# First products of the first layer from x without token factors, its norms reordered, and a down projection that ends in two halved tiles

## The chip, the cores and the metric

The kernel runs on one core of a Trainium2 chip. The metric is the device time of one execution in microseconds (us). The engines of the core are TensorE (PE: matrix products, with its weight loads listed as PEld), VectorE (DVE), ScalarE (ACT), GpSimd (POOL) and SyncE (SP, which here only starts transfers). Each engine works through its own list of instructions in order, and they wait for one another by semaphores.

## The reference

Two layers of an encoder over 512 tokens of width 1024, with 256 memory tokens. Cut to what matters here:

```
def rms_norm(x, g):
    y = x * rsqrt(mean(x * x, axis=-1) + 1e-6)
    return y * g

mem_n = rms_norm(mem, mem_norm_g)
for l in range(2):
    h = rms_norm(x, g_pre_mix[l])
    proj = h @ w_in[l]                    # 44 tiles of 128 columns
    q_a, k_a, v_a, q_b, k_b, v_b, q_m, gate_pre = split(proj)
    o_a = neighbourhood attention; o_b = dilated attention
    o_m = attention of q_m into mem_n @ w_mem_kv[l]
    merged = sum of sigmoid(gate) * (o @ w_br) over the three branches
    x = x + rms_norm(merged @ w_out[l], g_post_mix[l])
    h = rms_norm(x, g_pre_ffn[l])
    a, b = halves of conv3(h @ w_up[l])
    x = x + rms_norm((gelu(a) * b) @ w_down[l], g_post_ffn[l])
```

The norm of a token is one factor for the token (r, from the mean of its squares) times one gain for each channel (g). The factor may be applied before a product with weights or, as a scaling of columns, after it.

## The kernel before

Everything is kept transposed: x is 8 tiles of 128 channels x 512 tokens, and the tokens are worked on in two halves of 256 where a norm is near. Every product is made of three, since each float32 operand is split into a high part (hi, a rounding done as a cast on ACT) and a low part (lo, the rest, a subtraction on DVE or POOL): hi x hi, hi x lo, lo x hi (`mm3`, line 244). So each tile of weights (8 x 128 x 128, 512 KB) costs a load on SP's queue into one of three buffers (wraw), a cast on ACT (whi) and a subtraction on DVE or POOL (wlo), and each normalised tile of x costs on DVE a product with factor and gain, on ACT a cast and on DVE a subtraction (`normed`, line 340).

The order of work comes from `Woven` (line 46): PE's instructions are written out in one sequence with a clock that adds an estimated cost for each; other work is written as generator jobs that are due so many microseconds of that clock later, and `tick`, `need` and `give` let jobs in at their time or until a flag is set. So numbers such as KVD = 7.3 or LAT1 = 12.0 decide where in the lists of the engines a job's instructions stand.

What matters of the program, in order:

- Start of layer 0 (lines 835 to 848): load x's first half, two tiles of w_in, x's second half; norm of the first half; then squares of the second half, the other four tiles of the group, and the memory's norm (`mem_norm_job`, line 415) as a job.
- The group: the first six tiles of w_in (0, 3, 6, 1, 4, 7) are multiplied in pairs into six PSUM banks, first for tokens 0 to 255, then for 256 to 511 (`run_group`). Each pair of a half waits for one flag per half.
- Layer 0 then makes the memory's keys and values (`mem_kv`, four tiles of w_kv, line 442), and goes on to the projections of 512 columns, attention, gates, output projection, up projection with convolution and GELU.
- The down projection (`sublayer_end`, line 779): 8 output tiles m0 to m7, each 22 steps of three products. In layer 0, m0 to m6 are made for all 512 tokens, m7 in two halves, so that the norm of the first half can begin while the second half is multiplied. `end_job` (line 373) then scales the outputs og, adds them to x, and sums x's new squares in acc2; `pre_norm_job` of layer 1 follows (9 us of the clock later).
- The boundary to layer 1: `kv_ahead` (line 955) loads and splits w_kv's tiles and the first two of the group during m7; the memory's keys of layer 1 come behind m7; then layer 1's group.
- The memory's norm for layer 1 is spawned at the start of layer 0's down projection; its squares are made on ACT and added on POOL (MSQ = G).
- Some low parts are made on POOL: GEN = 'GGVGVG' and KVE = 'VVGG' name the engine of each group and key tile at the boundary (G is POOL, V is DVE); at the start the pairs (V, G) and (V, G, V, G) do.

In the profile line 114 is the helper through which all work of DVE and ACT is issued, so there the tiles' names tell the place. L242 is the matrix product, L253 a transpose, L192 the load of x, L225 a load of weights, L420 a load of memory tokens, L316 the addition of squares on POOL.

Of the kernel before, what the change touches and what calls it, by code (L numbers as in the profile page):

```python
# [7 lines left out]
F32 = mybir.dt.float32  # L8
# [8 lines left out]
N_MEM = 256  # L17
# [20 lines left out]
SQG, LOG, GEN, KVE = {0: (), 1: ()}, {0: (), 1: ()}, 'GGVGVG', 'VVGG'  # L38
# [4 lines left out]
KVD, GWD, NG, LAT1 = 7.3, 1.0, 2, 12.0  # L43
# [76 lines left out]
def tile_hybrid_encoder(ctx, tc, xT, memT, memg, vecs, rpb, w_in, w_kv, w_bra, w_brb, w_brm,  # L120
# [69 lines left out]
    def load_x(half):  # L190
        for k in range(0, KD, 2):
            nc.sync.dma_start(out=xs[k // 4][:, k % 4:k % 4 + 2, half], in_=xT[:, k:k + 2, half])  # L192

    load_x(HALVES[0])
# [27 lines left out]
    def weights(src, K, C, slot=None, eng=None, after=None):  # L222

        raw = wp.tile([128, K, C], F32, tag="wraw", name=nm("wraw"))
        nc.sync.dma_start(out=raw, in_=src)  # L225
# [119 lines left out]
    def raw_split(l, goff, k, src, hi, lo):  # L345

        g = vec[:, l, goff + k:goff + k + 1]
# [11 lines left out]
    def pre_norm_job(l, goff, acc, hs, i):  # L359
        half, box = HALVES[i], []  # L360
        yield from rstd_job(acc if isinstance(acc, list) else [acc[:, half]], 256, box)
        for k in range(KD):
            normed(x[k][:, half], vec[:, l, goff + k:goff + k + 1], box[0], hs[k][0][:, half], hs[k][1][:, half],
                   G if k in LOG[l > 0 and goff == V_PRE] else V)
        crit[0] = last_copy[0]
        yield 1.2
        wv.give(f"h{l}.{goff}.{i}")
# [5 lines left out]
    def end_job(l, goff, og, acc, acc2, i, then, lat, more=()):  # L373
        half, box = HALVES[i], []
        yield lat
        yield from rstd_job([acc[:, half]] + list(more), 256, box)
        for k in range(KD):
            V.tensor_mul(og[k][:, half], og[k][:, half], box[0])
            (G if then is None and i and k in TAILG else V).tensor_add(x[k][:, half], x[k][:, half], og[k][:, half])
            if acc2 is not None:  # L380
                sumsq_add(acc2[:, half], x[k][:, half], k == 0, None, G if k in SQG[goff == V_POSTF] else V)
            else:
                nc.sync.dma_start(out=out[:, k, half], in_=x[k][:, half])
        if then is not None:
            yield 9.0
            yield from then(i)

    def factor_end_job(l, goff, og, acc, acc2, i, nxt):
# [5 lines left out]
        for k in range(KD):  # L394
            V.tensor_mul(og[k][:, half], og[k][:, half], box[0])
            V.tensor_add(x[k][:, half], x[k][:, half], og[k][:, half])
            raw_split(l, gnext, k, x[k][:, half], h[k][0][:, half], h[k][1][:, half])
# [18 lines left out]
    def mem_norm_job(l, hm, slot):  # L416
# [5 lines left out]
        acc = small("h32", 3)  # L422
        for k in range(KD):
            sumsq_add(acc, raws[k], k == 0, None, MSQ if l else V)
        yield 14.0
        box = []
        yield from rstd_job([acc], N_MEM, box)
        for k in range(KD):
            t = slot(F32R, (128, 2, N_MEM))
            normed(raws[k], mg[:, k:k + 1], box[0], t[:, 0, :], t[:, 1, :])  # L430
            hm.append((t[:, 0, :], t[:, 1, :]))
        yield 1.2
# [11 lines left out]
    def mem_kv(l, hm, km, vm, pre=()):  # L444
        wv.need(f"mem{l}")
        for m in range(4):
            w = pre[m] if pre else weights(w_kv[l, m], KD, 128)
# [18 lines left out]
    def run_group(grp, hs, half, flag, cols=None, side=2):  # L466
        if flag and side == 2:
            wv.need(flag)
        n = len(hs)
        ws, pss = grp  # L470
        for i in range(0, len(ws), side):
            for k in range(n):
                if flag and side > 2:
                    wv.need(f"{flag}.{k}")
                rhs = [t[:, half] for t in hs[k]]
# [303 lines left out]
    def sublayer_end(l, goff, w_of, rhs, n_half, then, lat=(1.4, 1.8), mid=None, fill=()):  # L779
# [22 lines left out]
        ws = {m: [p() for p in w_of(m, m - n0)] for m in range(n0, KD)}  # L802
# [3 lines left out]
        for i, half in enumerate(HALVES):  # L806
            order = list(range(n0, KD) if i == 0 else range(KD - 1, n0 - 1, -1))
            while order:
# [26 lines left out]
    hs = h_tiles()  # L835
    wv.spawn(pre_norm_job(0, V_PRE, first_squares(HALVES[0]), hs, 0))
    gw = group_weights([w_in[0, m] for m in FIRST[:2]], (V, G))
# [229 lines left out]
```

## Time and profile before

| what | value |
|---|---|
| median of 3 runs | 1562.9 us (1562.28 to 1564.55) |
| the profiled execution | 1565.1 us |
| its span (first to last instruction) | 1563.3 us |
| mean granted PE clock | 0.994 |
| windows of 40 us with most idle PE: 0 to 40 | PE busy 27.47 us, clock 1.00 |
| 40 to 80 | PE busy 37.12 us, clock 1.00 |
| 640 to 680 | PE busy 36.98 us, clock 0.96 |
| 760 to 800 | PE busy 38.57 us, clock 0.96 |
| 800 to 840 | PE busy 34.63 us, clock 0.91 |

In what follows a row of the timeline reads: start, duration, engine, line, operation, output <- inputs by the program's names, shape, and how many such operations in a row were put together; brackets give the idle time of the engine just before it and which engine's result ended it. In the list of waits a row gives the total, the number and the longest. A row of the windows gives the stretch, its length, the busy time of PE, PEld, DVE, ACT and POOL with counts, then the granted PE clock (1.00 is full speed), the share of the DMA engines in use and the GB/s. A name like y, m, h or mm is a kind of buffer: mm, s, o and pt are PSUM banks, m and h split operands, y and acc float32 tiles of VectorE's size.

### The profile page before, as it was taken

To read this page: it belongs to the slowest core of one execution; us is meant where nothing else is said; L and a number is where in the kernel's file an instruction comes from. 1 tells how busy PE (TensorE), PEld (TensorE's weight loads), DVE (VectorE), ACT (ScalarE), POOL (GpSimd) and SP (SyncE) were. 2 spreads that over 40 slices of the span, in tenths; PEclk is the share of its full clock that TensorE was granted. 3 is DMA by queue.
4 is the path that set the end of the run, shared out by engine and by line. 5 is a ranking of instruction groups with operands and counts; after the bars stand their busy time and mean duration, and the time that the engine had idled before them with its cause. 6 is when DMAs were issued, how large, how long until landed. Compare 5 with 4: busy or idle time off the path is not lost.

```text
span 1563.3 us, 20698 instructions
## 1 busy us (share of the span) xinstructions
PE 1524.4 (98%) x7994; PEld 1303.7 (83%) x7994; DVE 945.2 (60%) x1682; ACT 735.1 (47%) x1267; POOL 155.2 (10%) x219
## 2 busy tenths in 40 slices
PE   6999999999999999999989999999999999999997
PEld 6888888888988888788889888888889888888887
DVE  6685566235777777742385856753456877775233
ACT  5564575236544444522344645743364544444231
POOL 4340000210000000100061400001100000000000
PEclk9999999999999999999989999999999999999999
DMA  7222113325113322333331221132250222333331
GB/s 244 88 79 72 61 57 96 93 95 163 54 56 101 100 94 95 104 98 101 115 115 44 80 69 63 56 108 81 95 189 15 81 95 95 94 100 96 98 103 63
DMA packets 46610, 144.90 MB, mean 93 GB/s; under 512 B 5232, under 2 KB 11376, under 8 KB 46512
## 3 DMA queue, kind: packets, MB, share of 16 engines
q1 hardware_dynamic: 44656, 139.61, 28.2%
q10 hardware_dynamic: 1152, 2.10, 0.5%
q0 software_dynamic: 704, 1.88, 0.4%
q8 instruction: 62, 1.02, 0.3%
q14 instruction: 36, 0.29, 0.1%
HBM read 141.47 MB, written 2.10 MB: 92 GB/s over the span
## 4 chain that ended last, share of the span: by engine, by line
PE 54%; DVE 3%; issue 0%; ACT 0%; ACTq 0%; DVEq 0%
PE mm L242 48%; PE s L242 3%; PE o L242 2%; PE pt L242 1%; PE pt L253 1%; DVE y L114 1%; DVE x L114 1%; DVE m L114 0%; DVE acc L114 0%; DVE wlo L114 0%; DVE ka L114 0%; DVE st L114 0%; ACT sq L114 0%; ACT y L114 0%; ACT m L114 0%
## 5 line engine op out<-in xcount | busy, mean ns | idle before, releaser
L242 PE MATMUL mm<-h,whi 128*128 128x512 f32 x2496 | 775.7, 392 | 0.0
L242 PEld LDWEIGHTS mm<-h,whi 128*128 128x128 f32 x2496 | 461.5, 188 | 90.9
L242 PE MATMUL mm<-h,wlo 128*128 128x512 f32 x1248 | 486.4, 390 | 0.0
L114 DVE TENSOR_TENSOR wlo<-wraw,whi 128x1024 fp32r<-128x1024 f32 (+1 forms) x213 | 259.8, 1221 | 293.9 <-ACT whi L114 291.5
L114 ACT CAST whi<-wraw 128x1024 fp32r<-128x1024 f32 (+1 forms) x213 | 221.0, 1039 | 318.5 <-PE mm L242 310.4
L242 PEld LDWEIGHTS mm<-h,wlo 128*128 128x128 f32 x1248 | 234.3, 188 | 49.9
L242 PE MATMUL mm<-m,whi 128*128 128x512 f32 (+1 forms) x800 | 216.3, 358 | 2.7 <-ACT whi L114 1.8
L242 PEld LDWEIGHTS mm<-m,whi 128*128 128x128 f32 x800 | 142.5, 190 | 25.1 <-ACT whi L114 2.2
L242 PE MATMUL mm<-m,wlo 128*128 128x512 f32 (+1 forms) x400 | 142.8, 357 | 1.2 <-DVE wlo L114 1.2
L114 DVE SCALAR_TENSOR_TENSOR y<-y,vec,y 128x511 f32<-128x511 f32 x176 | 130.9, 750 | 3.5 <-ACT y L114 0.9
L114 DVE TENSOR_TENSOR y<-mm,R 128x512 f32<-128x512 f32 x82 | 56.4, 688 | 68.5 <-PE mm L242 68.5
L242 PEld LDWEIGHTS mm<-m,wlo 128*128 128x128 f32 x400 | 75.9, 190 | 12.5 <-DVE wlo L114 1.6
L766 POOL TENSOR_TENSOR m<-m,y 128x512 f32<-128x512 f32 x28 | 36.1, 1288 | 405.7 <-DVE y L114 405.7
L114 ACT ACTIVATE y<-y,vec 128x512 f32<-128x512 f32 x88 | 71.0, 813 | 2.2 <-DVE y L114 1.9
L242 PE MATMUL mm<-m,m 128*128 128x512 f32 x240 | 63.6, 395 | 0.0
L114 ACT ACTIVATE y<-y 128x512 f32<-128x512 f32 x44 | 27.8, 632 | 72.0 <-DVE y L114 71.5
L242 PE MATMUL s<-h,m 128*128 128x256 f32 x384 | 54.7, 290 | 5.4 <-DVE m L114 5.4
L114 ACT ACTIVATE y<-mm,vec 128x512 f32<-128x512 f32 (+1 forms) x91 | 57.4, 631 | 0.1
L242 PE MATMUL mm<-h,m 128*128 128x256 f32 x360 | 54.6, 298 | 2.8 <-DVE h L114 1.8
L114 ACT CAST m<-pt 128x512 fp32r<-128x512 f32 (+1 forms) x72 | 38.2, 539 | 40.4 <-PE pt L253 32.0
L114 DVE TENSOR_TENSOR acc<-acc,sq 128x256 f32<-128x256 f32 (+1 forms) x80 | 40.5, 507 | 26.2 <-ACT sq L114 24.6
L114 DVE TENSOR_TENSOR m<-pt,m 128x512 fp32r<-128x512 f32 (+1 forms) x72 | 45.0, 629 | 18.3 <-ACT m L114 17.4
(143 smaller groups left out, 1762.5 us busy)
## 6 DMA issues: line engine op xcount, KB each, us to landing
wraw<-in_w_in_dram SPq DMA_DIRECT2D x88, 512.0 KB, 3.4
wraw<-in_w_up_dram SPq DMA_DIRECT2D x88, 512.0 KB, 3.3
wraw<-in_w_down_dram SPq DMA_DIRECT2D x32, 512.0 KB, 3.5
wraw<-in_w_out_dram SPq DMA_DIRECT2D x16, 512.0 KB, 4.2
wraw<-in_w_down_dram SPq DMA_DIRECT2D x16, 384.0 KB, 3.1
wraw<-in_w_kv_dram SPq DMA_DIRECT2D x8, 512.0 KB, 4.4
wraw<-in_w_bra_dram SPq DMA_DIRECT2D x16, 192.0 KB, 2.3
x<-in_xT_dram SPq DMA_DIRECT2D x8, 256.0 KB, 6.9
```

The costliest lines, as they stand in the source:

```text
L114: return op(*args, **kw)
L242: wv.pe(nc.tensor.matmul(ps, a, b, start=first, stop=last), cost)
L253: wv.pe(nc.tensor.transpose(ps[:, 128 * i:128 * i + 128], s, ident), 0.11)
L766: (V if br == 2 and m >= 6 else G).tensor_add(acc[m], acc[m], gs)
```

## The change

At the start of layer 0, x's first half is multiplied into the six banks straight from g x x (gain g, no token factor). `raw_split` makes high and low parts of g x x as each load lands, into tiles xg; the gains come by a small load of their own (g0) on ACT's queue. The first two weights and x are loaded in half-size pieces in turn. The second half is normed as before (`first_norm_job(1)`), the first half's norm is started inside the second's: its factor goes into R, and the six banks are multiplied by R (ones for the second half) with `scaled` when the group has ended. The normed first half is then used by the later projections. The memory's norm waits for the flag "norm0" that the first half's norm gives at its end, and the memory's keys come behind the group. All splits at the start and at the boundary are given to DVE (GEN, KVE, the pairs).

At the down projection of layer 0, n_half becomes 2 with again=True: m0 to m5 for all tokens, then m6 first half (weights streamed), m7 first half, m7 second half, m6 second half, for which m6's weights are loaded and split once more. The memory's norm job of layer 1 is spawned with a delay of 20.0; KVD goes from 7.3 to 22.3; `end_job` yields 1.0 for each tile and 1.0 instead of 9.0 at its end; the group of a layer waits for a flag per tile of x (h{l}.{goff}.{i}.{k}).

```
-SQG, LOG, GEN, KVE = {0: (), 1: ()}, {0: (), 1: ()}, 'GGVGVG', 'VVGG'
+SQG, LOG, GEN, KVE = {0: (), 1: ()}, {0: (), 1: ()}, 'VVVVVV', 'VVVV'
-KVD, GWD, NG, LAT1 = 7.3, 1.0, 2, 12.0
+KVD, GWD, NG, LAT1 = 22.3, 1.0, 2, 12.0
...
+    g0 = const.tile([128, KD], F32, name="g0")
+    nc.scalar.dma_start(out=g0, in_=vecs[:, 0, V_PRE:V_PRE + KD])
...
-    def raw_split(l, goff, k, src, hi, lo):
+    def raw_split(g, src, hi, lo):
         ACT.activation(hi, src, AF.Copy, scale=g)
         V.scalar_tensor_tensor(out=lo, in0=src, scalar=g, in1=f32(hi), op0=ALU.mult, op1=ALU.subtract)
...
     def end_job(l, goff, og, acc, acc2, i, then, lat, more=()):
-        yield lat
+        yield lat if then is None else ready(lat)
...
                 sumsq_add(acc2[:, half], x[k][:, half], k == 0, None, G if k in SQG[goff == V_POSTF] else V)
+                yield 1.0
...
-            yield 9.0
+            yield 1.0
...
     def mem_norm_job(l, hm, slot):
-        acc = small("h32", 3)
+        acc = acctile()[:, 0:N_MEM]
         for k in range(KD):
             sumsq_add(acc, raws[k], k == 0, None, MSQ if l else V)
-        yield 14.0
+        yield 14.0 if l else "norm0"
...
             hm.append((t[:, 0, :], t[:, 1, :]))
+            yield 0.9
...
+            while again and order:
+                m = order.pop(0)
+                if m == n0:
+                    one(m, mmbank((128, 256)), w_of(m, None), half, False)
+                    continue
+                if m not in ws:
+                    ws[m] = [p() for p in w_of(m, m - n0 - 1)]
+                ps = mmbank((128, 256))
+                run_group(([sum(ws[m], [])], [ps]), rhs, half, None, slice(0, 256))
+                post_norm_tile(l, goff, m, ps, og, acc, half, False)
...
+    def first_norm_job(i, R):
+        half, box = HALVES[i], []
+        if i == 1:
+            sqs.append(first_squares(half))
+            yield ready(2.0)
+        yield from rstd_job(sqs[-1], 256, box)
+        if i == 0:
+            ACT.copy(R[:, half], box[0])
+        for k in range(KD):
+            normed(x[k][:, half], g0[:, k:k + 1], box[0], hs[k][0][:, half], hs[k][1][:, half])
...
+            if i == 1 and k == 3:
+                sqs.append(first_squares(HALVES[0]))
+        if i == 1:
+            wv.spawn(first_norm_job(0, R), ready(0.5))
+        else:
+            wv.give("norm0")
...
+    load_x(HALVES[1])
+    wv.spawn(first_norm_job(1, R), 9.0)
+    pss = group_banks()
+    run_group((gw, pss[:2]), xg, FULL, None, HALVES[0])
+    gw += group_weights([w_in[0, m] for m in FIRST[4:]], (V, V))
...
+    run_group((gw[2:], pss[2:]), xg, FULL, None, HALVES[0])
+    wv.spawn(mem_norm_job(0, hm, big), 6.0)
+    run_group((gw, pss), hs, HALVES[1], f"h0.{V_PRE}.1")
...
+        if l == 0:
+            wv.need(f"h0.{V_PRE}.0.{KD - 1}")
+            pss = [scaled(ps, R) for ps in pss]
+            mem_kv(0, hm, km, vm, kv)
...
-            wv.spawn(mem_norm_job(l + 1, hm, htile))
+            wv.spawn(mem_norm_job(l + 1, hm, htile), 20.0)
...
-            sublayer_end(l, V_POSTF, w_of, fs, 1, then, (1.4, LAT1), lambda: wv.spawn(kv_ahead()))
+            sublayer_end(l, V_POSTF, w_of, fs, 2, then, (1.4, 1.8), lambda: wv.spawn(kv_ahead()), again=True)
```

Three places of the engines' lists show what moves. First, PE around the memory's norm in layer 0. Before, the mean (pt_542) stands inside the group's first pair for the second half, and its spread (pt_542 <- ident) soon after in the second pair:

```order
L242 MATMUL mm_278<-h_121,m_162 128x256
L242 MATMUL mm_278<-h_120,m_163 128x256
L242 MATMUL pt_542<-mean,h_94_387 128x1 x2
L242 MATMUL mm_277<-h_122,m_152 128x256
L242 MATMUL mm_277<-h_123,m_152 128x256
```

In the changed kernel the group's last product (pt_203) is followed at once by the mean of the memory (pt_699), its spread, and the first product for the memory's keys (mm_747):

```order
L250 MATMUL pt_203<-h_120,m_268 128x256
L250 MATMUL pt_203<-h_121,m_268 128x256
L250 MATMUL pt_203<-h_120,m_269 128x256
L250 MATMUL pt_699<-mean,acc_503 128x1 x2
L250 MATMUL pt_699<-ident,st_702 128x128 x2
L250 MATMUL mm_747<-m_707,whi_657 128x256 x2
```

The mean of the memory waits there for the first half's norm on DVE, and the spread for DVE's reciprocal, ahead of which stand the six scalings by R:

```order
L114 TENSOR_TENSOR y_695<-o_202,R_122 128x512
L114 TENSOR_TENSOR y_697<-pt_203,R_122 128x512
L114 RECIPROCAL st_702<-st_702 128x2
L114 SCALAR_TENSOR_TENSOR ka_897<-y_689,ka_895 64x512
L114 SCALAR_TENSOR_TENSOR ka_898<-y_689,ka_896 64x512
L114 COPY sq_915<-y_691 128x8x8
L114 SCALAR_TENSOR_TENSOR h_126_708<-m_495,mg,pt_699 128x256
```

So the memory's norm has moved from beside the group's products to behind them.

Second, ACT at the head of layer 0's down projection. Before, the last squares of the memory tokens (sq from h_6081, h_6083), three of which wait for POOL, stand ahead of the cast of the second piece of weights (whi_6131):

```order
L114 ACTIVATE sq_1210_6096<-h_6081 128x256 [waits DMAHW7_49]
L114 ACTIVATE sq_1211_6099<-h_6081 128x256 [waits Pool_49]
L114 ACTIVATE sq_1212_6102<-h_6083 128x256 [waits DMAHW0_49,Pool_49]
L114 ACTIVATE sq_1213_6105<-h_6083 128x256 [waits Pool_49]
L114 CAST ka_6057<-y_6045 128x512 [waits DVE_49]
L114 CAST whi_6131<-wraw_6129 128x1024 [waits DMAHW2_49,PE_49]
```

In the changed kernel that cast (whi_6143) stands ahead of the squares, and those that wait for POOL behind the evacuation of the first tile (acc_6114, y_6106):

```order
L114 CAST whi_6143<-wraw_6141 128x1024 [waits DMAHW5_49,PE_49]
L114 ACTIVATE sq_1235_6250<-h_6240 128x256 [waits DMAHW7_49]
...
L114 CAST whi_6230<-wraw_6228 128x1024 [waits DMAHW4_49,PE_49]
L114 ACTIVATE acc_6114<-mm_6116 128x512 [waits PE_49]
L114 ACTIVATE y_6106<-mm_6116,vec 128x512
L114 ACTIVATE acc_6248<-h_6240 128x256
L114 ACTIVATE sq_1239_6262<-h_6244 128x256 [waits Pool_49]
```

The squares have moved behind four casts of weights.

Third, DVE at the end of the down projection in the changed kernel. The second pass of m6 adds three splits (wlo_7014, wlo_7064, wlo_7134), which stand between the first half's additions to x (x_85, x_86), the sums of its squares (acc_6115), and the splits of w_kv's tiles (m); the piece around the last one reads:

```order
L114 TENSOR_TENSOR wlo_7064<-wraw_7061,whi_7063 128x1024
L114 TENSOR_TENSOR acc_6115<-acc_6115,sq_1354_7055 128x256
L114 TENSOR_TENSOR m_7073<-wraw_7070,m_7072 128x512
L114 TENSOR_TENSOR y_6112<-y_6112,pt_6932 128x256
L114 TENSOR_TENSOR m_7077<-wraw_7070,m_7076 128x512
L114 TENSOR_TENSOR x_86<-x_86,y_6112 128x256
L114 TENSOR_TENSOR y_6113<-y_6113,pt_6932 128x256
L114 TENSOR_TENSOR m_7097<-wraw_7094,m_7096 128x512
L114 TENSOR_TENSOR acc_6115<-acc_6115,sq_1363_7088 128x256
L114 TENSOR_TENSOR m_7101<-wraw_7094,m_7100 128x512
L114 TENSOR_TENSOR x_86<-x_86,y_6113 128x256
...
L114 TENSOR_TENSOR wlo_7134<-wraw_7131,whi_7133 128x768
```

Before, none of these three splits existed, and two of the four tiles of w_kv were split on POOL.

More of the change, by code (lines that the diff above doesn't have):

```diff
@@ L472, in run_group @@
             for k in range(n):
-                if flag and side > 2:
+                if flag:
                     wv.need(f"{flag}.{k}")
-                rhs = [t[:, half] for t in hs[k]]
+                rhs = [t if half == FULL else t[:, half] for t in hs[k]]
                 for w, ps in zip(ws[i:i + side], pss[i:i + side]):
@@ L801, in sublayer_end @@
                 fill[m]()
-        ws = {m: [p() for p in w_of(m, m - n0)] for m in range(n0, KD)}
+        ws = {} if again else {m: [p() for p in w_of(m, m - n0)] for m in range(n0, KD)}
         if mid is not None:
```

94 lines of the change are left out of this document (64 added, 30 removed).

## The prediction

> **What bounds the kernel now.** I read the page first: span, busy time, slices.
>
> ```profile
> span 1563.3 us, 20698 instructions
> ...
> PE 1524.4 (98%) x7994; PEld 1303.7 (83%) x7994; DVE 945.2 (60%) x1682; ACT 735.1 (47%) x1267; POOL 155.2 (10%) x219
> ...
> PE   6999999999999999999989999999999999999997
> ```
>
> TensorE (PE) is busy for 1524.4 of 1563.3 us, so a change can gain only in the 38.9 us in which PE stands still, or where its clock is low. The slices put most of that into the first one and the one at 780 to 820 us. The list of PE's waits names them.
>
> ```profile
> PE pt L242 <- DVE y L114: 9.0, 1, 9.0
> PE s L242 <- DVE m L114: 5.4, 1, 5.4
> ...
> PE mm L242 <- ACT whi L114: 1.8, 1, 1.8
> ...
> PE pt L242 <- DVE acc L114: 1.4, 1, 1.4
> PE mm L242 <- DVE wlo L114: 1.2, 1, 1.2
> ```
>
> The 9.0 is the start, the 1.8 and 1.2 lie at the head of layer 0's down projection, the 1.4 and 5.4 at the layer boundary. These are the three places that the change touches, and I price each from the timelines there.
>
> **Place 1, head of the down projection.** PE, ACT and POOL in the timeline (start, duration, engine, operation, count, and in brackets the idle time before it):
>
> ```profile
> 655.84 0.61 PE L242 MATMUL mm<-m,whi 128*128 128x512 f32 x2
> ...
> 656.52 0.61 PE L242 MATMUL mm<-m,whi 128*128 128x512 f32 x2
> ...
> 658.28 7.45 POOL L316 TENSOR_TENSOR h<-h,sq 128x256 f32<-128x256 f32 x7 [301.60 <-ACT sq L114]
> ...
> 661.34 0.42 ACT L114 ACTIVATE sq<-h 128x256 f32<-128x256 f32 x1 [0.72 <-POOL h L316]
> ...
> 662.17 1.77 ACT L114 CAST whi<-wraw 128x1024 fp32r<-128x1024 f32 x2
> ...
> 663.26 0.74 PE L242 MATMUL mm<-m,whi 128*128 128x512 f32 x2 [1.81 <-ACT whi L114]
> ...
> 665.20 0.50 PE L242 MATMUL mm<-m,wlo 128*128 128x512 f32 x1 [1.20 <-DVE wlo L114]
> ...
> 676.08 0.62 PE L242 MATMUL mm<-m,whi 128*128 128x512 f32 x2
> ```
>
> Read it backwards: PE waits for a cast of weights (whi), the cast stands behind ACT's last squares of the memory tokens, and those wait for POOL, whose seven additions take 7.45 us. A down tile is 22 steps of three products, and a step takes 656.52 - 655.84 = 0.68 us, so the tile should take 15.0 us. It took 676.08 - 655.84 = 20.24. The difference, 5.2 us, is 3.0 of waiting and 2.2 of low clock behind it. In the changed order of ACT (shown above) that cast stands ahead of all the squares, and the squares that wait for POOL stand behind the tile's evacuation. Nothing else takes the cast's place: the four squares that remain in between cost about 4 x 0.4 = 1.6 us at a time when ACT is not waited for. I take **-5.2 us**; if the next piece's cast is late by as much as DVE's split was, 1.2 us, and the clock falls once (1.7, below), about 2.9 of it stays: bounds -5.2 and -2.3.
>
> **Place 2, the start.** PE and DVE:
>
> ```profile
> 9.04 1.84 PE L242 MATMUL pt<-mean,y 128*128 128x1 f32 x8 [9.04 <-DVE y L114]
> ...
> 13.66 0.58 PE L242 MATMUL mm<-h,m 128*128 128x256 f32 x1 [1.01 <-ACT h L114]
> ...
> 37.16 5.20 PE L242 MATMUL mm<-h,m 128*128 128x256 f32 x42
> ...
> 56.49 0.40 PE L242 MATMUL mm<-m,whi 128*128 128x256 f32 x2
> ...
> 69.59 0.63 PE L242 MATMUL mm<-h,whi 128*128 128x512 f32 x2
> ```
>
> ```profile
> 18.13 0.47 DVE L114 SCALAR_TENSOR_TENSOR h<-x,vec,pt 128x256 f32<-128x256 f32 x1
> 18.52 0.41 DVE L114 TENSOR_TENSOR h<-h,h 128x256 fp32r<-128x256 f32 x1
> 18.86 0.47 DVE L114 SCALAR_TENSOR_TENSOR h<-x,vec,pt 128x256 f32<-128x256 f32 x1
> ...
> 20.31 0.68 DVE L114 TENSOR_TENSOR m<-wraw,m 128x512 fp32r<-128x512 f32 x1
> 20.91 0.41 DVE L114 TENSOR_TENSOR h<-h,h 128x256 fp32r<-128x256 f32 x1
> ...
> 786.19 0.41 DVE L114 TENSOR_TENSOR acc<-acc,sq 128x256 f32<-128x256 f32 x1
> 786.52 0.41 DVE L114 TENSOR_TENSOR x<-x,y 128x256 f32<-128x256 f32 x1
> ```
>
> Now: first product 13.66, the six-tile group ends and the memory keys begin at 56.5, the first full-width projection starts at 69.6; the last is the mark I compare, since from there both kernels run alike. Prices: a 256-wide product 5.20/42 = 0.124 us; a normalised tile costs DVE 18.86 - 18.13 = 0.73 us, a 128x512 operation 20.91 - 20.31 = 0.60, a 128x256 addition 786.52 - 786.19 = 0.33; consecutive operations overlap by some 0.07.
>
> Gain first. The changed group needs only x times g and weights. The first load and the memory's loads in the records of ACT, and the rate over 0 to 16 us in 40 slices:
>
> ```profile
> 3.51 1.42 ACT L114 ACTIVATE y<-x 128x256 f32<-128x256 f32 x4 [1.26 <-DMA x<-in_xT_dram]
> ...
> 29.88 0.38 ACTq L420 DMA_DIRECT2D m<-in_memT_dram  x1
> ...
> 34.91 0.42 ACT L114 ACTIVATE h<-m 128x256 f32<-128x256 f32 x1 [0.84 <-DMA m<-in_memT_dram]
> ```
>
> ```profile
> GB/s 0 0 0 0 38 200 361 374 397 183 80 257 239 309 281 362 402 405 394 397 410 399 369 341 338 379 371 379 364 384 382 397 369 261 82 31 10 0 0 164
> ```
>
> From about 5 us on the loads run at some 380 GB/s, so bytes set the start: the first halves of two weights (0.75 MB with x) are there at about 6 to 7, the third and fourth weight (3 MB in all with their x) at 10 to 14, the fifth and sixth behind x's second half at 15 to 19. First product about 8, first pair of tiles ended 11 to 12, second pair 19, third pair, held by the split of the sixth weight behind twelve squares on ACT, about 27.5. That is some 9 us ahead of before, whose first half ended at 37.2.
>
> Then it is spent. The memory loads are issued from ACT's queue inside the third pair, at about 22.5, and land 34.91 - 29.88 = 5.0 us later at the most; six squares of memory and a DVE addition stand **ahead of the second half's norm** on ACT and DVE. So that half's first pair starts near 30 and is fed at DVE's pace, 8 steps with weights' splits and memory additions between, to about 38; two pairs of 5.9 us follow: group end about **50.3**, 6 us ahead of 56.5.
>
> Now the memory norm. In the order shown above, PE has nothing between the group's last product and the memory's mean. On DVE the first half's norm (16 operations, 8 x 0.73) starts near 46 and ends near 52, with the scalings of the six banks (6 x 0.60) about 55.5; then comes the memory's reciprocal, the 1.0 of ACT's root and PE's spreading, three evacuations and the first normalised memory tile: first key product about 57.9. PE idles 50.9 to 57.9. The first key tile is then paced by DVE, 8 x 0.73, to 64.0, and three tiles of 24 x 0.12 = 2.9 us follow: mark at about 72.8 against 69.6. So **+3.2 us**: 6 gained, 9 given back, where the old order had the memory norm hidden beside the group's second half. Bounds: group end at 47.5 gives 70 - 69.6 = +0.4, and with the first half's norm started earlier -1; group end at 52 and a halved clock behind the gap gives +6.
>
> **Place 3, the layer boundary.** PE, the clock, and one row of the page:
>
> ```profile
> 775.41 0.40 PE L242 MATMUL mm<-m,whi 128*128 128x256 f32 x2
> ...
> 784.17 3.04 PE L242 MATMUL mm<-h,h 128*128 128x256 f32 x24
> ...
> 791.52 0.58 PE L242 MATMUL pt<-mean,acc 128*128 128x1 f32 x4 [1.43 <-DVE acc L114]
> ...
> 812.91 7.13 PE L242 MATMUL s<-h,m 128*128 128x256 f32 x45 [5.37 <-DVE m L114]
> ...
> 843.79 0.63 PE L242 MATMUL mm<-h,whi 128*128 128x512 f32 x2
> ```
>
> ```profile
> 793.00:794.00 1.00, 1.00 (x7) 1.00 (x6) 0.43 (x1) 0.26 (x1) 1.00 (x3) 0.50 0.00 0
> ...
> 796.00:797.00 1.00, 1.00 (x10) 1.00 (x10) 1.00 (x4) 0.07 (x1) 0.94 (x3) 1.00 0.97 365
> ```
>
> ```profile
> L114 DVE TENSOR_TENSOR wlo<-wraw,whi 128x1024 fp32r<-128x1024 f32 (+1 forms) x213 | 259.8, 1221 | 293.9 <-ACT whi L114 291.5
> ```
>
> Before, two stalls (1.43 and 5.37 us), and after the first the granted clock was 0.50 at 793 and 1.00 again at 796. Behind the second, 45 products took 7.13 us where 45 x 0.12 = 5.4 would do: a drop costs **1.7 us**.
>
> After: m6 and m7 in halves. PE adds 66 x (2 x 0.12 - 0.227) = 0.9 us, since a 512-wide product takes 0.68/3. Half 0's sum is complete at 768.5, 6.9 us earlier (a half tile is 66 x 0.12 = 7.9), since both second halves now follow it. Count time from the start of m7's second half, 768.5 (775.41 less 7.9 is where m7 began before, plus 0.9). DVE's chain (shown above) is then solid from 4.25. Nine 256-wide operations and a 1024-wide split (1.22 less the overlap, 1.15): the low weights of m6's first piece are ready at 4.25 + 3.0 + 1.15 = 8.4, in time for its start at 7.9 plus two products. Eight 256-wide, two 512-wide and a split later, 13.5: the second piece, wanted after eight steps of 0.36 and a mean between them, at 11.8, so PE waits 1.7. Seven, six and a 768-wide split (three quarters, 0.87) later, 20.3: the third, wanted eight steps after 13.5, at 16.4, so 3.9. Its load, one of three that m6's second pass adds on SP's queue, waits for a free buffer, but should be there before DVE is. m6 ends at 22.3; the memory keys take 13.2, as four tiles of 2.9 with the means between, to 35.5. The six weights' splits are off POOL and the per-tile flags let the group start on the first normalised tile, so the 5.37 us goes. Half 1's x, counted along DVE the same way, has its mean 2.0 us late, near 48. Six half pairs of 5.9 and this wait: group end about 73.0, that is 841.5 against 843.8: **-2.3 before clock**. The first stall's low clock lies under the next wait; the other two stalls should each bring a drop, by the 1.43 us row: +3.4. So **+1.1**; bounds -2.3 and +3.5.
>
> The Trainium skill, in "TensorE: Matmul & The Clock Gate" ("The two states you'll see"), has the clock halve after an idle window of about 3.4 us. Here 1.43 us was enough, so the measurement decides. By the page only the 3.9 us stall would drop the clock, and place 3 would be -0.6.
>
> **Sum.** -5.2 + 3.2 + 1.1 = -0.9 us against this execution's 1565.1. The median of the runs is 1562.9, 2.2 lower; I carry the difference over: **1562.0 us**. A measurement tells about 0.2%, 3.1 us, from no change.
>
> **Rivals.** (A) Faster: DVE is ready earlier. If the first half's norm runs inside the second pair instead of behind the third, and DVE is no longer stretched by POOL at the boundary, the start costs 0 and the boundary gives its -2.3: -5.2 + 0 - 2.3 = -7.5, 1555.4. For it: POOL's share of DVE's slowness goes with its splits. Against it: DVE's order puts memory additions and key weights ahead of that norm.
>
> (B) Slower: the memory norm behind the group. Price: PE idle from the group's end to the first key product plus a DVE-paced key tile, with a halved clock. It decides if that idle time exceeds about 9 us: start +6, boundary +3.5, head -5.2, hence +4.3, 1567.2. For it: nothing covers PE there. Against: key tiles starved by DVE hide a low clock.
>
> (C) It doesn't do what it says: the loads, halved and led by a small load of g, land no earlier, the first product stays near 13, and the group ends at 55: start +7, sum +3, 1565.9. Against: bytes ahead of the first product fall from over 1.5 MB to 0.75.
>
> **Chances.** Forecast 0.45, A 0.30, B 0.17, C 0.08. The forecast's own bounds of about 3.5 either way put 0.08 of it on faster and 0.05 on slower; of C half is slower. Faster 0.37 (0.29 of A and 0.08), slower 0.26 (B, 0.04 of C, 0.05), same 0.37. The range reaches from A's time less 1.4 to B's plus 0.8: 1554 to 1568.
>
> **What would show it.** Right: no wait of 1.8 near 661 and a first down tile of 15 us; first product near 8; group end near 50 and a PE gap of about 7 us before the keys; the mark at 72.8; two new waits on low weights (wlo) of 1.7 and 3.9 in m6's second half. Wrong: a gap under 4 us at the keys (A), or a mark beyond 75 (B), or the first product behind 12 (C); or a new wait between the places, where the order of PE's rows is the same in both kernels and I count nothing.

## The result, and the profile after

The changed kernel takes 1575.2 us (median of 4 runs, 1574.91 to 1576.6) against 1562.75 us for the kernel before: ratio 1.0072, 95% interval 1.006 to 1.0085. It is **slower by some 12 us**, where 1562.0 us (no change) was forecast with a range up to 1568. The profiled executions are 9.8 us apart (1565.1 and 1574.91); the profiled one of before lay 2.35 us above its median.

The page of the changed kernel, first its span and busy times, then the slices of PE and its clock:

```profile
span 1573.1 us, 20847 instructions
...
PE 1530.6 (97%) x8060; PEld 1310.7 (83%) x8060; DVE 955.6 (61%) x1718; ACT 742.1 (47%) x1281; POOL 131.9 (8%) x202
...
PE   7899999999999999999979999999999999999997
...
PEclk9899999999999999999989999999999999999999
```

PE idles 1573.1 - 1530.6 = 42.5 us instead of 38.9, and is busy for 6.2 us longer at a lower mean clock (0.989 instead of 0.994). Its list of waits:

```profile
PE mm L250 <- ACT m L114: 7.9, 3, 5.2
PE s L250 <- DVE m L114: 5.2, 1, 5.2
PE pt L250 <- DVE st L114: 4.2, 2, 3.7
PE mm L250 <- ACT whi L114: 3.1, 1, 3.1
...
PE mm L250 <- DVE wlo L114: 2.0, 2, 1.8
```

The longest wait of the first row is the start (5.2 instead of 9.0). The second row, 5.2, was to go and is still there. The third, with 3.7 as its longest, is new: the memory's norm behind the group. The last two are m6's second pass, new.

I cut both traces at the same instructions; this ledger adds up to the 9.8 us. The cuts are the first 512-wide projection of layer 0 and of layer 1, the first product of layer 0's down projection, of m6, of layer 1's memory keys, and of the group's second pair.

| stretch | before | after | difference | forecast |
|---|---|---|---|---|
| start to first projection | 69.59 | 76.84 | +7.25 | +3.2 |
| to the down projection | 586.25 | 586.27 | 0.0 | 0 |
| m0 to m5 | 96.60 | 91.37 | -5.23 | -5.2 |
| m6 and m7 | 31.73 | 41.68 | +9.95 | +1.1 for this and the next two |
| keys and the group's first pair | 22.84 | 19.50 | -3.34 | |
| rest of the group | 36.78 | 37.57 | +0.79 | |
| layer 1's projections to the end | 719.51 | 719.87 | +0.36 | 0 |

The rows behind the start, PE and DVE of the changed kernel:

```profile
5.16 1.32 PE L250 MATMUL mm<-m,m 128*128 128x256 f32 x3 [5.16 <-ACT m L114]
...
14.77 5.92 PE L250 MATMUL s<-m,m 128*128 128x256 f32 x48
...
31.69 7.28 PE L250 MATMUL mm<-h,m 128*128 128x256 f32 x43 [2.35 <-ACT h L114]
...
47.68 0.60 PE L250 MATMUL pt<-ident,st 128*128 128x128 f32 x4
...
52.80 0.52 PE L250 MATMUL pt<-h,m 128*128 128x256 f32 x3
54.11 0.58 PE L250 MATMUL pt<-mean,acc 128*128 128x1 f32 x4 [0.79 <-DVE h L114]
58.35 1.22 PE L250 MATMUL pt<-ident,st 128*128 128x128 f32 x4 [3.66 <-DVE st L114]
61.30 0.58 PE L250 MATMUL mm<-m,whi 128*128 128x256 f32 x1 [1.73 <-ACT m L114]
...
76.84 0.63 PE L250 MATMUL mm<-h,whi 128*128 128x512 f32 x2
```

```profile
48.73 1.26 DVE L114 SCALAR_TENSOR_TENSOR h<-x,g,pt 128x256 f32<-128x256 f32 x3 [1.92 <-ACT R L114]
...
57.54 0.68 DVE L114 TENSOR_TENSOR y<-pt,R 128x512 f32<-128x512 f32 x1
58.14 0.15 DVE L114 RECIPROCAL st<-st 128x2 f32<-128x2 f32 x1
...
60.34 1.25 DVE L114 SCALAR_TENSOR_TENSOR h<-m,mg,pt 128x256 f32<-128x256 f32 x3
```

The products do start early, at 5.2 instead of 13.7. The group ends at 53.2, 3.3 us ahead of before. Then PE has nothing to do until the six scalings (57.54 is the last) let DVE come to the memory's reciprocal (58.14) and first tile (60.34): the first key product is at 61.3, where before it was at 56.5: 4.8 us of the 7.25. The other 2.4 lie in the keys, which take 15.5 us instead of 13.1; the granted clock was 0.51 on the mean of 56 to 66.

The rows of the boundary, PE and ACT, and three windows:

```profile
784.56 0.39 PE L250 MATMUL mm<-m,wlo 128*128 128x256 f32 x1 [1.75 <-DVE wlo L114]
...
791.59 0.79 PE L250 MATMUL mm<-ka,whi 128*128 128x256 f32 x2 [3.10 <-ACT whi L114]
...
821.37 1.01 PE L250 MATMUL s<-h,m 128*128 128x256 f32 x3 [5.19 <-DVE m L114]
```

```profile
790.71 0.83 ACT L114 CAST whi<-wraw 128x768 fp32r<-128x768 f32 x1 [0.51 <-DMA wraw<-in_w_down_dram]
```

```profile
785.00:786.00 1.00, 1.00 (x11) 1.00 (x10) 1.00 (x3) 0.00 (x0) 0.00 (x0) 1.00 0.80 307
786.00:787.00 1.00, 1.00 (x7) 1.00 (x6) 1.00 (x3) 0.48 (x1) 0.00 (x0) 0.51 0.94 291
...
795.00:796.00 1.00, 1.00 (x7) 1.00 (x7) 0.12 (x1) 0.00 (x0) 1.00 (x9) 0.50 0.55 209
```

Two waits in m6's second pass, and half clock from 786 to 796. The cast of the last piece waited for its load, which SP had issued behind the loads of key tiles and of a tile of the group:

```profile
779.38 4.04 SPq L227 DMA_DIRECT2D wraw<-in_w_kv_dram  x2
784.53 0.33 SPq L227 DMA_DIRECT2D wraw<-in_w_in_dram  x1
786.40 0.33 SPq L227 DMA_DIRECT2D wraw<-in_w_down_dram  x1
```

### The profile page after: what moved, and what is told of

Its sections match the earlier page's. It is cut to its first block, busy times and chain, and to the rows that moved or that the text cites. A ratio compares the mean times of both kernels' runs of the same rounds, so it can differ in the third digit from the quotient of the medians.

```text
span 1573.1 us, 20847 instructions
## 1 busy us (share of the span) xinstructions
PE 1530.6 (97%) x8060; PEld 1310.7 (83%) x8060; DVE 955.6 (61%) x1718; ACT 742.1 (47%) x1281; POOL 131.9 (8%) x202
## 4 chain that ended last, share of the span: by engine, by line
PE 89%; DVE 4%; ACT 1%; DMA 1%; issue 0%; ACTq 0%
PE mm L250 79%; PE s L250 4%; PE o L250 3%; PE pt L261 2%; DVE m L114 1%; PE pt L250 1%; DVE y L114 1%; DVE wlo L114 1%; DMA wraw<-in_w_down_dram 0%; DVE ka L114 0%; ACT whi L114 0%; DMA wraw<-in_w_in_dram 0%; DVE x L114 0%; ACT y L114 0%; ACT m L114 0%
## 5 line engine op out<-in xcount | busy, mean ns | idle before, releaser
L250 PE MATMUL mm<-m,whi 128*128 128x512 f32 (+1 forms) x832 | 220.6, 353 | 2.4 <-ACT m L114 1.7
L250 PEld LDWEIGHTS mm<-m,whi 128*128 128x128 f32 x832 | 147.9, 191 | 24.1 <-ACT m L114 2.0
L250 PE MATMUL mm<-m,wlo 128*128 128x512 f32 (+1 forms) x416 | 146.3, 352 | 1.8 <-DVE wlo L114 1.8
L250 PEld LDWEIGHTS mm<-m,wlo 128*128 128x128 f32 x416 | 79.8, 192 | 12.5 <-DVE wlo L114 2.2
L250 PE MATMUL mm<-m,m 128*128 128x512 f32 (+1 forms) x288 | 72.4, 387 | 6.1 <-ACT m L114 6.1
L250 PEld LDWEIGHTS mm<-m,m 128*128 128x128 f32 x288 | 51.6, 197 | 15.2 <-ACT m L114 6.4
L114 DVE TENSOR_TENSOR m<-wraw,m 128x512 fp32r<-128x512 f32 (+1 forms) x74 | 48.8, 674 | 24.5 <-ACT m L114 24.1
L114 ACT CAST m<-pt 128x512 fp32r<-128x512 f32 (+1 forms) x72 | 38.0, 540 | 40.3 <-PE pt L261 31.6
L114 ACT CAST m<-y 128x512 fp32r<-128x512 f32 (+1 forms) x36 | 22.3, 619 | 72.6 <-DVE y L114 72.5
```

The costliest lines, as they stand in the source:

```text
L114: return op(*args, **kw)
L250: wv.pe(nc.tensor.matmul(ps, a, b, start=first, stop=last), cost)
```

## The experiments

Each changes few lines of one of the two kernels. The table has the same cuts; where m6 is whole its 15.08 us are counted to "m6 and m7". Ratios are to the kernel before, measured beside each. Its own median lay between 1562.75 and 1565.33 us in these comparisons, so times of runs from two comparisons are not compared to better than some 2.5 us; the stretches of the table are each from one profiled execution.

| run | ratio (95%) | start | m0 to m5 | m6, m7 | keys, first pair | rest of group |
|---|---|---|---|---|---|---|
| before | 1 | 69.59 | 96.60 | 31.73 | 22.84 | 36.78 |
| changed | 1.0072 (1.006, 1.0085) | 76.84 | 91.37 | 41.68 | 19.50 | 37.57 |
| e1 | 0.9961 (0.9949, 0.9974) | 69.96 | 91.37 | 31.74 | 22.84 | 36.77 |
| e2 | 0.9996 (0.9984, 1.0007) | 69.62 | 97.42 | 31.73 | 22.85 | 35.88 |
| e3 | 1.0068 (1.0049, 1.0087) | 78.99 | 96.58 | 31.73 | 21.37 | 37.01 |
| e4 | 1.0018 (1.0009, 1.0028) | 70.45 | 91.38 | 41.00 | 19.45 | 37.50 |
| e5 | 1.0057 (1.0042, 1.0072) | 78.77 | 91.38 | 41.10 | 19.44 | 36.14 |
| e6 | 1.0046 (1.0031, 1.0061) | 75.28 | 91.37 | 41.41 | 20.25 | 36.08 |
| e7 | 1.0044 (1.0028, 1.0061) | 77.34 | 91.38 | 34.15 | 29.00 | 31.66 |
| e8 | 1.0008 (0.9999, 1.0017) | 76.19 | 91.36 | 31.74 | 22.83 | 36.62 |
| e9 | 0.9956 (0.9943, 0.9968) | 69.25 | 91.36 | 31.74 | 25.80 | 31.97 |
| e10 | 0.9986 (0.9977, 0.9995) | 72.46 | 91.36 | 31.74 | 22.83 | 36.87 |
| e11 | 0.9967 (0.9955, 0.998) | 69.56 | 91.37 | 31.73 | 25.77 | 33.71 |
| e12 | 0.9985 (0.9976, 0.9994) | 71.22 | 91.36 | 31.74 | 25.79 | 31.97 |
| e13 | 1.0033 (1.002, 1.0046) | 68.87 | 91.37 | 42.52 | 26.26 | 31.49 |
| e14 | 0.9942 (0.9925, 0.9959) | 69.80 | 91.37 | 31.76 | 21.20 | 33.62 |

### The parts alone: e1, e3, e4

**e1**, late squares in the kernel before:

```
-            wv.spawn(mem_norm_job(l + 1, hm, htile))
+            wv.spawn(mem_norm_job(l + 1, hm, htile), 20.0)
```

> The kernel before with one number changed: the second memory norm is spawned 20.0 later at the head of the down projection. Theory (POOL-bound squares ahead of a weight cast cost 5.2 us): no wait of 1.81 us on whi near 661, first down tile 15.0 us instead of 20.24, whole kernel about 5.2 us faster, near 1557.6. Rival (the gain needs the rest of the change): less than 2 us.

Median 1558.41 against 1565.33, as the theory had it: the 5.2 us lie inside the interval of the ratio. ACT of e1 at the place:

```profile
657.82 1.03 ACT L114 CAST whi<-wraw 128x1024 fp32r<-128x1024 f32 x1
658.76 0.41 ACT L114 ACTIVATE h<-h 128x256 f32<-128x256 f32 x1
```

The cast is ahead of the squares, the stretch falls by 5.2 us, and no other stretch moves by more than 0.4. The one number gives this whole part.

**e3**, the changed start on the rest of the kernel before (`first_norm_job`, xg and g0 as in the change):

```
-    wv.spawn(pre_norm_job(0, V_PRE, first_squares(HALVES[0]), hs, 0))
...
+    wv.spawn(first_norm_job(1, R), 9.0)
+    run_group((gw, pss[:2]), xg, FULL, None, HALVES[0])
...
-        yield 14.0
+        yield 14.0 if l else "norm0"
```

> The kernel before with the changed start alone (first half from g times x, its norm inside the second's, memory norm and keys behind the group); head of the down projection and boundary as before. Theory (the three places add up: start +7.25 by the first full-width projection, 69.59 before and 76.84 after): 7 us slower, near 1570, and the wait of 1.8 at 660 plus 7 still there. Rival (the start's loss is made up or enlarged later): 3 us or less, or over 10.

Median 1574.89 against 1565.33: 0.68% slower, 9.4 us in the start and next to nothing made up later. The same start took 76.84, 78.99, 78.77 and 77.34 in four kernels (changed, e3, e5, e7), so its length varies by 2 us; it is 7 to 9 us longer than before in each.

**e4**, the changed kernel with the start of before:

```
-    run_group((gw, pss[:2]), xg, FULL, None, HALVES[0])
...
+    wv.spawn(pre_norm_job(0, V_PRE, first_squares(HALVES[0]), hs, 0))
...
-        yield 14.0 if l else "norm0"
+        yield 14.0
```

> The changed kernel with the start of before: late squares, halved m6 and m7, all splits at the boundary on DVE. Theory (head of the down projection -5.2, boundary +7.4): 2 to 3 us slower than before, near 1565; first full-width projection of layer 1 about 2.2 us later than before's 843.8. Rival (the boundary's loss in the changed kernel comes from the shifted start, for example a different phase of the clock or of loads): -4 us or better.

Median 1567.79 against 1565.33, 0.18% slower: -5.2 from the squares, +6.6 from the boundary (41.00 + 19.45 + 37.50 against 91.35). The boundary loses by itself, whatever the start.

### The boundary: e2, e5, e7, e13, e14

**e2**, other order of banks in layer 1's group, on the kernel before:

```
-        return [mmbank(), mmbank(), sbank(), sbank(), obank(128), tbank()]
+        a, b, c, d, e, f = mmbank(), mmbank(), sbank(), sbank(), obank(128), tbank()
+        return [a, b, e, f, c, d] if late else [a, b, c, d, e, f]
...
-        pss = group_banks()
+        pss = group_banks(l == 1)
```

> The kernel before, only the order of the six banks of layer 1's group changed: the pair of banks o and pt is multiplied second, the pair s and s third. Theory (the 5.37 us wait of the second pair is a wait for a bank s that a job of the memory values still holds until DVE has split it, and not for the group's weights): the wait is gone or under 1.5 us, with the low clock behind it 6 to 7 us faster, near 1556. Rival (the second pair waits for its weights' low parts on DVE): the wait stays at 4 to 6 us on the other pair, time within 1 us of before.

Each theory has one half right. The wait of the second pair is gone though its weights are the same, so it was the bank: in the kernel before it ended with DVE's split of the memory values out of a bank s, not with a split of weights. That split stood behind two additions to x on DVE, which took 1.82 us while POOL split weights:

```profile
810.61 1.82 DVE L114 TENSOR_TENSOR x<-x,y 128x256 f32<-128x256 f32 x2
810.79 1.36 POOL L220 TENSOR_TENSOR m<-wraw,m 128x512 fp32r<-128x512 f32 x1 [1.71 <-ACT m L114]
...
812.35 0.41 DVE L114 TENSOR_TENSOR m<-s,m 128x256 fp32r<-128x256 f32 x1
...
812.91 1.41 PE L242 MATMUL s<-h,m 128*128 128x256 f32 x5 [5.37 <-DVE m L114]
```

But the time did not fall (ratio within 0.9984 to 1.0007), since a second wait stood behind the first. PE of e2:

```profile
818.62 0.99 PE L242 MATMUL pt<-mean,acc 128*128 128x1 f32 x4 [3.65 <-DVE acc L114]
```

The mean of the second half stands in PE's order before DVE has summed that half.

**e5**, the same two lines in the changed kernel:

> The changed kernel with the banks o and pt multiplied second in layer 1's group, s and s third. Theory (bank wait removed, but DVE's update of x's second half is a second wait behind it, as the run of the kernel before with this order showed): the 5.2 us wait of the second pair goes, a wait on the mean of the second half of 2 to 4 us appears, time 1 to 3 us less than the changed kernel, 1572 to 1574. Rival (weights' splits on DVE bind): nothing gained.

Median 1574.71 against 1564.84 of before in that comparison, +9.9 where the changed kernel had +12.4; but the two were not measured side by side. In the trace the wait for the bank is gone, a wait of 3.93 us on the mean of the second half stands in its place, as the theory had it, and the rest of the group fell by only 1.4 us.

**e7**, in the changed kernel, so that m6's second-pass weights stand ahead of three key tiles:

```
-KVD, GWD, NG, LAT1 = 22.3, 1.0, 2, 12.0
+KVD, GWD, NG, LAT1 = 26.0, 1.0, 2, 12.0
```

> The changed kernel with KVD 26.0 instead of 22.3: m6's second-pass weights stand ahead of three of the four key tiles in the queue of loads and on DVE. Theory (m6's two waits of 1.75 and 3.1 and the half clock between them come from the key tiles' loads and splits ahead of its own): both waits under 0.6, m6 ends 6 us earlier; part comes back as a wait of the keys for their tiles, so 2 to 6 us faster. Rival (DVE is full there in any order): the waits reappear in the keys in full, within 1.5 us of the changed kernel.

PE of e7:

```profile
786.22 0.39 PE L250 MATMUL mm<-ka,wlo 128*128 128x256 f32 x1 [0.52 <-DVE wlo L114]
...
816.69 1.02 PE L250 MATMUL pt<-mean,acc 128*128 128x1 f32 x4 [7.85 <-DVE acc L114]
```

Median 1571.95 against 1564.84. m6 and m7 fall from 41.68 to 34.15, and the granted clock is 1.00 from 784 to 798: both waits and the half clock came from the queue ahead of m6's weights. Half of that is given back, not in a wait of the keys for their tiles, as the theory had it, but in one of 7.85 us for DVE's sum of the second half: the boundary (the last three columns) is 94.81 against 98.75 and before's 91.35.

**e13** and **e14** tell the two changes at the boundary apart: halves without the moved splits, moved splits without halves.

```
e13, on e4:  -GEN, KVE = 'VVVVVV', 'VVVV'    +GEN, KVE = 'GGVGVG', 'VVGG'
e14, on e1:  -GEN, KVE = 'GGVGVG', 'VVGG'    +GEN, KVE = 'VVVVVV', 'VVVV'
```

> The start of before, late squares, halved m6 and m7, with the splits of four group tiles and two key tiles at the boundary on POOL again. Theory (the halves' second pass of weights, queued with the key tiles, costs the time, on whichever engine the key tiles are split): half m6 to keys 38 us or more (16.65 + 15.08 + 7.9 if nothing waited is 31.7 with m6 whole, 41.0 in the run with VectorE), boundary still 4 us or more over before. Rival (VectorE is overfull because POOL's splits came to it): under 35 us from half m6 to keys, boundary within 2 us of before.

> The kernel before with the late squares and all splits at the boundary on VectorE, m6 whole, m7 alone halved. Theory (the halves cost the time): within 3 us of the late squares alone (5 to 6 us faster than before, so 2 to 8 faster). Rival (the splits on VectorE cost the time): 4 us or more slower than the late squares alone.

e13: 1570.08 against 1564.63, its PE:

```profile
776.29 0.39 PE L249 MATMUL mm<-m,wlo 128*128 128x256 f32 x1 [1.76 <-DVE wlo L114]
783.19 0.80 PE L249 MATMUL mm<-ka,whi 128*128 128x256 f32 x2 [4.01 <-ACT whi L114]
```

The same two waits with the splits on POOL: the **halves cost the time**, with what goes along with them (m6's second load of weights, KVD, the yields of `end_job`, a flag per tile), and not the engine of the splits. How much each of these costs was not told apart, but for KVD in e7.

e14: 1554.95 against 1564.63, 0.58% (0.41 to 0.75%) faster than before, the lowest ratio of all; its interval overlaps those of e1 and e9. The splits on DVE do not cost but gain: in the traces its boundary is 86.6 us against 91.3 in e1, 4.8 less; by the medians, each against before beside it, e14 gains 9.7 us and e1 6.9, some 3 us apart. In e14 PE waits 2.30 us for the bank s in place of 5.37:

```profile
803.14 5.63 PE L242 MATMUL s<-h,m 128*128 128x256 f32 x45 [2.30 <-DVE m L114]
```

DVE's split out of that bank starts at 802.58 instead of 807.44 in e1. In e1 three operations of DVE ahead of it (two additions to x, one to acc) took 1.5 us each instead of 0.41, each while POOL split a tile of weights, some 3.2 us more in all; in e14 there are no such splits on POOL, and the operations there took 0.41 or 0.42. So part of the 5.37 us was POOL's splits after all, by way of DVE and the bank.

### The start: e6, e8, e10

**e6**, the memory's norm ahead of the first half's, in the changed kernel, and **e8**, the same start with late squares and the boundary of before:

```
-        yield 14.0 if l else "norm0"
+        yield 14.0 if l else f"h0.{V_PRE}.1.{KD - 1}"
...
-            wv.spawn(first_norm_job(0, R), ready(0.5))
+            wv.spawn(first_norm_job(0, R), ready(0.5) + 7.0)
```

> The changed kernel with the memory's norm of layer 0 placed behind the second half's norm and ahead of the first half's norm (in DVE's order 16 operations swapped), nothing else. Theory (PE idles before the keys because the memory's norm stands last on DVE): the gap before the first key product falls from about 8 to about 2 us, the keys run unstarved, first full-width projection at 67 to 69 instead of 76.8, whole kernel 8 to 9 us faster, near 1566. Rival (the start is bound by DVE's total work, whatever its order): the projection starts at 74 or later, 3 us or less.

> The start of the changed kernel with the memory's norm ahead of the first half's, the late squares, and the boundary of the kernel before. Theory (places add up): start -1 to -2, head of the down projection -5.2, so 6 to 7 us faster than before. Rival (the early start gains nothing even so): 5 us or less, the gain of the late squares alone.

e6 took 1572.95 against 1564.84 and e8 1565.85 against 1564.84, so in e8 the rival held. PE of e6:

```profile
56.28 0.48 PE L250 MATMUL mm<-m,whi 128*128 128x256 f32 x2
...
67.97 0.39 PE L250 MATMUL mm<-m,wlo 128*128 128x256 f32 x1 [3.52 <-DVE wlo L114]
...
75.28 0.63 PE L250 MATMUL mm<-h,whi 128*128 128x512 f32 x2
```

The gap before the keys is gone (first product 56.3 instead of 61.3), yet the projection comes only 1.6 us earlier: the third key tile's split now stands behind the first half's norm and the scalings. The rival was nearer; the wait moved.

**e10**, on e8, with the first half's mean inside the group's last pair, and the memory's normalised tiles let in more closely:

```
-            if not l:
-                yield 0.9
+            if not l:
+                yield 0.4
...
-            wv.spawn(first_norm_job(0, R), ready(0.5) + 7.0)
+            wv.spawn(first_norm_job(0, R), ready(0.5) + 3.5)
```

> The changed start with the memory's norm ahead of the first half's, as in the run before it, and the first half's mean moved from behind the group into its last pair, so that DVE has no 5 us hole there; late squares, old boundary. Theory (DVE's work of the start fits beside the group once nothing waits behind it): keys' waits of 1.7 and 3.5 us shrink to under 1.5 in all, first full-width projection at 68 to 70 instead of 76.2, whole kernel 6 to 8 us faster than before. Rival (the early start costs DVE more than the group's time holds): projection at 72 or later, 4 us or less.

1563.13 against 1565.12 (0.14% faster, 0.05 to 0.23%); projection at 72.5, so the rival held. The key waits are 1.30 and 1.93 us. So more than half of the start's loss was order, and the rest is still there. Up to the projection DVE is busy for 50.9 us in e10 (51.6 in the changed kernel) and for 46.4 before, which is on the rival's side. With the late squares of e1 alone the kernel is faster than with this start added.

### Attempts to go further: e9, e11, e12

**e9**, on e1: the first half's mean later at the boundary.

```
-            yield 9.0
+            yield 9.0 if i else 11.5
```

> The kernel before with the late squares and the first half's mean of new squares 2.5 us later in PE's order (9.0 becomes 11.5 for that half). Theory (a PE wait of 1.43 us costs 1.43 plus about 1.7 of half clock, and the mean is ready some 7.4 us behind the keys' start): no wait at that mean, clock 1.00 through the keys, 2 to 3 us less than the late squares alone, so 8 to 9 us faster than before. Rival (DVE's update of x sets the group's start anyway): the 5.4 us wait of the second pair grows by what is saved, under 1 us gained.

1557.91 against 1565.12. Keys and group together take 57.8 us against 59.6 in e1: 1.8 us gained in the traces, between the two theories. By the medians, each against before beside it, e9 gains 7.2 us and e1 6.9, which the noise does not tell apart. The 1.43 us wait is gone and that for the bank s is 2.06 instead of 5.37, but there are new ones:

```profile
786.13 2.77 PE L242 MATMUL mm<-h,m 128*128 128x256 f32 x21 [1.52 <-ACT y L114]
798.86 1.01 PE L242 MATMUL pt<-ident,st 128*128 128x128 f32 x4 [2.81 <-ACT m L114]
807.08 5.63 PE L242 MATMUL s<-h,m 128*128 128x256 f32 x45 [2.06 <-DVE m L114]
```

**e11** adds e2's order and a later mean of the second half; **e12** is e10 with e9's line.

```
e11, on e9:  -            yield 9.0 if i else 11.5
             +            yield 13.0 if i else 11.5
```

> Late squares, first half's mean 2.5 us later, banks s and s multiplied last, second half's mean 4 us later. Theory (the second pair's wait is a bank, the wait behind it is DVE's sum of the second half, some 34 us behind the keys' start): the bank wait goes, the mean's wait is 1 to 2 us instead of 3.65, another 1 to 3 us less than with the first half's mean alone. Rival (DVE's sum comes later still, or the second half's norm is then waited for): same time or more.

> The start with both norms inside the group, the late squares, the first half's mean later at the boundary. Theory (places add up): the sum of the two gains above, 8 to 11 us faster than before. Rival: no more than the better of the two.

e11 took 1559.5 and e12 1561.98, both against 1565.12: the rivals held. In e11 the rest of the group took 33.71 us instead of 31.97, and in e12 the start, 1.6 us longer than before, took back most of the 1.9 us that the boundary gained.

## Why the prediction was wrong

- **Head of the down projection: right.** -5.2 forecast, -5.23 measured, and e1 shows that one number gives it.
- **Start: the way forecast, the size wrong.** The early group is paid back where the memory's norm stands behind it, as forecast, but the term was +3.2 and measured +7.25, outside its bounds of -1 and +6. The mis-sized step is the start of the first half's norm on DVE: put near 46, it came at 48.7. Its mean stood at 45.4 in PE's order, behind products of the second half that began at 31.7 and not near 30; and the 1.92 us of idle DVE in its row are PE's spread of the factor (up to 48.3) and ACT's copy of R (0.37 us), which I had left out. So the first key product came at 61.3 and not at 57.9. The keys took 15.5 us where 14.9 was forecast. The group's end was put at 50.3 and came at 53.2, since the first pair of tiles ended at 14.8 and not at 11 to 12, and the second half's first pair at 40.3 and not near 38; the first mean and spread stood between the products too.
- **Boundary: the step "the 5.37 us goes" failed.** It was to go because the weights' splits leave POOL and the group can start on the first normalised tile. But it is a wait for a PSUM bank (e2), which PE gets only when DVE has split the memory values out of it. With m6 whole, the moved splits shorten it to 2.30 (e14); in the bundle with the halves it cost 5.19 again instead of 5.4 us less. Nor would 5.4 us have been gained by the bank alone, since the mean of the second half stands next (e2, e5). The 2.0 us that I counted for that mean did not come: the wait for the bank stood ahead of it.
- **"The first stall's low clock lies under the next wait" failed too.** The first wait came as forecast (1.75 for 1.7). The second was near in size (3.1 and 0.2 for 3.9) by luck: the last piece was late by its load and not by DVE, against "it should be there before DVE is". The clock, still 1.00 behind the first wait, fell at 786 and stayed at 0.50 through the second and for the six steps behind it, to 796: m6 ended 25.4 us after the mark and not 22.3. From there to the group's end it took 57.1 us and not 50.7. These 9.5 us, less the 3.4 that were counted for the clock, are what the boundary cost beyond its +1.1, to within 0.2. The chain on DVE was priced well: its start at 4.25, for which the working shows no row, came at 4.3, and the second piece's low weights, forecast for 13.5, at 13.8.
- **Rival B** (slower, by the memory's norm behind the group and the boundary's stalls) had the sign, and 0.17 of the chances. One of its signs came, a mark beyond 75 (76.84), and so did the low clock that it priced. Its time was 1567.2, and its turning point, over 9 us of idle PE, was not met: PE was idle for 0.79 + 3.66 + 1.73 = 6.2 us. **Rival A** was wrong in its first half: the first half's norm could not run inside the second pair while its mean stood at the end of that pair in PE's order. Its other half, DVE no longer stretched by POOL at the boundary, is seen in e14, where the boundary gains, but m6 is whole there. **Rival C** was wrong: the first product came at 5.2.
- Not settled: of the start's remaining loss in e10 (72.5 against 69.6) the runs do not tell how much is DVE's longer work and how much its order. At the boundary they do not tell the halving from its second load of weights: a halved m6 with its weights kept and not loaded again was not tried.

## What to carry to other kernels

A wait names the instruction that ended it: look at that row's output and inputs before calling it by the work around it. Here m<-s was the emptying of a bank and not a split of weights; ask what stands ahead of that instruction on its engine before counting on an edit. Before a removed wait is counted as gained, ask which wait stands next in the same engine's order (e2, e6, e7: each wait taken away came back, in part or nearly whole, at a later row that needs DVE), and test the parts of a bundle apart: one number of this change was worth 5.2 us and the engine of the splits another 3 to 5 us, while the rest of the bundle cost 7 at the start and, with its second load of weights, as much at the boundary.

## What the runs showed of the hardware

A short idle time of PE is not always followed by half clock. In the kernel before, one of 1.43 us was (0.50 at 793); in e9 waits of 1.52 and 2.06 us, and in e14 one of 2.30 us, were followed by full clock, while a wait of 2.81 us in e9 was followed by half clock again (0.50 from 800 to 802). Windows of e9 behind its 2.06 us wait, granted clock in the third column from the end:

```profile
807.00:808.00 1.00, 0.93 (x8) 0.95 (x9) 1.00 (x4) 0.31 (x1) 0.00 (x0) 1.00 0.96 381
808.00:809.00 1.00, 1.00 (x11) 1.00 (x10) 1.00 (x4) 0.11 (x1) 0.00 (x0) 1.00 0.57 230
```

In the changed kernel the clock fell only at about 786, over a microsecond after the wait of 1.75 us had ended at 784.6. The Trainium skill, "TensorE: Matmul & The Clock Gate" (section "The two states you'll see"), calls the window of about 3.4 us in which activity is judged free-running. That waits of similar length fall on either side agrees with it; that 1.43 us can be enough does not agree with its figure of one idle window.

Some operations of DVE take longer while POOL works. Between 752 and 844 of the kernel before, an addition to x (128x256) took 0.41 us on the mean of the 4 that ran with POOL idle and 0.81 on the mean of the 12 that overlapped with its work, 1.5 at most; the products y<-y,pt, which read a PSUM bank, took 0.41 in both cases.
